# A hybrid token-mixer layer on one core: its opening loads and turns the first token tile earlier, and starts two gates together

## The chip, the core and the metric

The kernel runs on one core of a Trainium2 chip. The metric is the device time of one execution in microseconds (us), the median of the runs shown; lower is better. The core has a matrix engine (TensorE, PE in the profile; its weight loads are the row PEld), a vector engine (VectorE, DVE), an engine for activation functions (ScalarE, ACT), a general engine (GpSimd, POOL) and an engine that only issues transfers (SyncE, SP). Each works through its own instructions in order. Transfers between the chip's main memory and SBUF are issued by an engine's queue and carried out by 16 DMA engines. PE writes to a second on-chip memory, PSUM, in banks of 128 x 512 numbers of 32 bits.

## The reference, cut to what matters

Two groups of tokens, 2048 sample tokens and 128 prompt tokens of width 1024, pass through one layer with shared weights. Around the change the reference computes

```
m = silu(cvec) @ w_ada + b_ada          # one conditioning vector per group, w_ada is 1024 x 3072
shift, scale, gate = split(m, 3)
xn = rmsnorm(h, ln_g) * (1 + scale) + shift
proj = xn @ w_in                        # 7696 columns: qkv, beta, dec, z_a, u_b, v_b, z_b, x_c, z_c, gates
```

and later uses silu(z_a), 512 columns of the projection, as the gate of the first mixer branch. Behind it stand that branch (a gated DeltaNet in both directions in chunks), a spatial gating branch, a Fourier branch, the projections that merge them, the output projection, a gated residual and a last norm.

## The kernel before, in words

All large products are made of three products of 16-bit numbers: each operand is held as a high and a low half (`w.hi`, `w.lo`; `xh`, `xl`), and hi x hi, hi x lo and lo x hi are summed in PSUM. The scaled and shifted tokens are kept on chip, transposed (channels on the partitions), as `xh` and `xl`. Tokens are worked in five tiles (`TBS`): four of 512 sample tokens, numbered 0 to 3, and one of 128 prompt tokens; the contraction over 1024 channels runs in 8 steps of 128 (`KT`).

**The modulation** (L398 to L411). `w_ada`'s columns for shift and scale come in 8 blocks of 256 columns, each as two loads of 512 KB (tile `ast`, 8 buffers). PE multiplies them by the two conditioning vectors (`mm` at L161); in the blocks 0, 2, 4 and 6 (`AD`) the second half is summed by VectorE instead (`ada_sum`, L380 and L382) and then added over partitions by PE with the selector `sel`. The result, 2 x 256, is copied out (L409) and turned to columns by PE (L411) in the PSUM tile `pa`. Behind block 3 (`XB = 4`) the load of the first token tile (`load_x`, L389, 2 MB) and the small parameters (`columns`, L355 to L363) are issued. With all eight blocks there, L415 to L426 add the bias, form `ms` (scale) and `sh` (shift), derive from bounds on both a power-of-two factor `sx` and its inverse `isx` (`scales`, L178 to L188, whose PE matmul at L181 adds over the partitions), and multiply by it.

**A weight block** of 128 columns (512 KB, tile `wst`, two buffers) is loaded by `read_w` (L195) and converted by `converting` (L198 to L219): ScalarE squares it with a sum (L209), VectorE casts the sum (L175), PE adds it over partitions (L181), VectorE forms the factor (L183 to L187) and `w.inv`, the product of the inverse factor and `isx` (L216), ScalarE writes `w.hi` (L218) and VectorE `w.lo` (L219). `wlist` holds the order of the blocks, the four of z_a first; `weight_step` takes one step of the conversion in hand, `fetch` raises the count that may be begun, `getw` steps until blocks are done and `read_next` issues a load ahead.

**A token tile** (L438 to L466). ScalarE squares its rows with sums (L447), VectorE and GpSimd form the reciprocal root (L170, L171), VectorE scales the rows (L451). For each k PE transposes four 128 x 128 blocks (L455) into a bank, VectorE scales and shifts them to the 32-bit tile `xm` (L457), ScalarE casts that to `xh` (L458), GpSimd subtracts to `xl` (L459). Then for each of the four z_a blocks `gemm_T` (L230) runs the 8 steps of three matmuls, ScalarE takes a sigmoid (L464), VectorE the product (L465), and the result goes to main memory one group late (L467). The next stage is the q, k and v projection with its convolution.

**What sets the order.** A scheduler orders every engine's instructions ahead of the run by simulating their time, with the program's order as priority. `tc.high_priority()` raises it; `tc.issue_after(i)` keeps instructions behind the instruction i in that order. On the chip each engine then follows its fixed order and waits on semaphores. SP's queue holds nearly all loads of the opening. A tile taken from a pool waits until the last use of the buffer that it takes over.

## Time and profile before

| what | value |
|---|---|
| median of 3 runs | 2199.03 us (2198.21 to 2199.14) |
| span of the profiled execution, first to last instruction | 2198.9 us |
| the same execution's time around the span | not shown apart from the runs' times; the median is 0.1 us above the span |
| PE busy in the span | 2133.4 us, 97% |
| DVE, ACT, POOL busy | 1297.7, 1007.5 and 713.8 us |
| mean granted PE clock | 0.994 |
| read from main memory, written | 234.67 MB, 127.62 MB |

Views used below: the page; a table by stretch (its length, then busy time of each engine with the count of instructions, the granted PE clock as a share of full speed, the mean busy share of the DMA engines and GB/s); instructions in order of time (start, length, engine, line, operation, output <- inputs, and in brackets the idle time before it and what ended it); groups of instructions by line and form (count, busy us, mean ns of one, idle time before and its cause); DMA issues (count, KB each, median us from issue to landing). PE's matmuls are pipelined, so the distance of two starts says more than the length of one.

### The profile page before, as it was taken

To read this page: it belongs to the slowest core of one execution; us is meant where nothing else is said; L and a number is where in the kernel's file an instruction comes from. 1 tells how busy PE (TensorE), PEld (TensorE's weight loads), DVE (VectorE), ACT (ScalarE), POOL (GpSimd) and SP (SyncE) were. 2 spreads that over 40 slices of the span, in tenths; PEclk is the share of its full clock that TensorE was granted. 3 is DMA by queue.
4 is the path that set the end of the run, shared out by engine and by line. 5 is a ranking of instruction groups with operands and counts; after the bars stand their busy time and mean duration, and the time that the engine had idled before them with its cause. 6 is when DMAs were issued, how large, how long until landed. Compare 5 with 4: busy or idle time off the path is not lost.

```text
span 2198.9 us, 41979 instructions
## 1 busy us (share of the span) xinstructions
PE 2133.4 (97%) x15990; PEld 1231.3 (56%) x15990; DVE 1297.7 (59%) x3085; ACT 1007.5 (46%) x2325; POOL 713.8 (32%) x861
## 2 busy tenths in 40 slices
...
GB/s 279 142 99 156 252 117 111 60 206 220 238 224 237 205 166 110 123 115 115 219 171 165 161 168 187 235 186 212 213 207 147 172 125 123 124 101 110 180 153 105
DMA packets 304275, 365.04 MB, mean 166 GB/s; under 512 B 39393, under 2 KB 215754, under 8 KB 302026
## 3 DMA queue, kind: packets, MB, share of 16 engines
...
q14 instruction: 76, 0.62, 0.1%
HBM read 234.67 MB, written 127.62 MB: 165 GB/s over the span
## 4 chain that ended last, share of the span: by engine, by line
PE 47%; DMA 6%; DVE 5%; ACT 3%; issue 1%; POOL 1%; SPq 0%; ACTq 0%; POOLq 0%; DVEq 0%
PE b L161 47%; DMA st<-br 2%; DMA wst<-in_w_branch_dram 1%; DMA wst<-in_w_in_dram 1%; DMA mt<-mrg 1%; DVE E L788 1%; DVE XB L787 1%; DMA ei<-XB 0%; DMA skn<-kv 0%; DMA br<-o 0%; ACT big L1336 0%; DMA XB<-nd 0%; ACT XB L793 0%; DVE big L1337 0%; DVE u L904 0%
## 5 line engine op out<-in xcount | busy, mean ns | idle before, releaser
L161 PE MATMUL b<-xh,whi 128*128 128x512 f16 (+1 forms) x1920 | 650.5, 347 | 7.7 <-DVE sg L1125 5.0
L161 PE MATMUL b<-xl,whi 128*128 128x512 f16 (+1 forms) x1920 | 650.8, 347 | 0.0
L161 PE MATMUL b<-xh,wlo 128*128 128x512 f16 (+1 forms) x1920 | 650.2, 347 | 0.4 <-DVE wlo L219 0.4
L161 PEld LDWEIGHTS <-whi 128*128 128x128 f16 x3904 | 356.4, 98 | 335.2 <-issue 13.7
L161 PEld LDWEIGHTS <-wlo 128*128 128x128 f16 x1952 | 191.1, 98 | 178.8 <-issue 1.3
L161 PE MATMUL b<-big,bhi 128*128 128x512 f16 (+1 forms) x960 | 250.5, 347 | 1.5 <-DVE big L1337 1.1
L1376 POOL TENSOR_TENSOR mrow<-mrow,sg 128x512 f32<-128x512 f32 (+1 forms) x80 | 95.0, 1187 | 288.4 <-DVE sg L1375 163.6
L161 PE MATMUL b<-big,blo 128*128 128x512 f16 (+1 forms) x480 | 163.3, 347 | 0.0
L1366 ACT ACTIVATE sg<-b,winv 128x512 f32<-128x512 f32 (+1 forms) x120 | 74.2, 619 | 153.9 <-PE b L161 153.4
L628 POOL TENSOR_TENSOR cy<-cy,raw 128x545 f32<-128x545 f32 (+1 forms) x48 | 74.5, 1580 | 184.4 <-ACT raw L627 184.4
L161 PEld LDWEIGHTS <-xh 128*128 128x128 f16 x1496 | 117.1, 98 | 29.9 <-issue 1.5
L161 PEld LDWEIGHTS <-bhi 128*128 128x128 f16 x960 | 87.0, 98 | 76.0 <-ACT big L1336 0.3
L175 DVE CAST wscb<-wss 128x1 bf16<-128x1 f32 x93 | 14.3, 154 | 190.9 <-ACT wlo L209 83.4
L1375 DVE SCALAR_TENSOR_TENSOR sg<-b,binv,sg 128x512 f32<-128x512 f32 (+1 forms) x80 | 53.4, 668 | 102.3 <-PE b L161 90.9
L860 POOL COPY T<-ES 32x256 f16<-32x256 f16 x68 | 28.5, 419 | 208.2 <-DMA ES<-ei 179.3
L161 PE MATMUL b<-whi,xl 128*128 128x128 f16 x544 | 93.0, 219 | 0.0
L161 PE MATMUL b<-whi,xh 128*128 128x128 f16 x544 | 93.0, 219 | 0.0
L161 PE MATMUL b<-wlo,xh 128*128 128x128 f16 x544 | 93.0, 219 | 0.0
L161 PE MATMUL b<-wohi,mh 128*128 128x512 f16 (+2 forms) x248 | 91.9, 372 | 0.6 <-ACT mh L1446 0.6
L161 PE MATMUL b<-wohi,ml 128*128 128x512 f16 (+2 forms) x248 | 91.7, 372 | 0.3 <-DVE ml L1447 0.3
L161 PE MATMUL b<-wolo,mh 128*128 128x512 f16 (+2 forms) x248 | 91.9, 372 | 0.0
L219 DVE SCALAR_TENSOR_TENSOR wlo<-wst,wsc,whi 128x1024 f16<-128x1024 f32 x52 | 72.4, 1396 | 31.6 <-ACT whi L218 31.3
(455 smaller groups left out, 4281.2 us busy)
## 6 DMA issues: line engine op xcount, KB each, us to landing
wst<-in_w_in_dram SPq DMA_DIRECT2D x60, 512.0 KB, 5.5
...
st<-br SPq DMA_DIRECT2D x48, 256.0 KB, 4.6
mrow<-mrg SPq DMA_DIRECT2D x18, 512.0 KB, 4.0
...
dc<-dec SPq DMA_DIRECT2D x17, 512.0 KB
kq<-qkv SPq DMA_DIRECT2D x34, 256.0 KB, 4.8
```

Source lines behind the costliest of these rows:

```text
L161: PE.matmul(out, l, r, start=start, stop=stop)
L175: V.tensor_copy(sb16, ss)
L219: V.scalar_tensor_tensor(w.lo, st, s, w.hi, ALU.mult, ALU.subtract)
L628: G.tensor_tensor(y[:, c0:c1], y[:, c0:c1], raw[:, 1 + c0:1 + c1], ALU.mult)
L787: V.tensor_tensor(t3, X3[:, 0:k, k:k + 1].to_broadcast([P, k, n_]), E3[:, k:k + 1, k:32].to_broadcast([P, k, n_]), ALU.mult)
L788: V.tensor_tensor(E3[:, 0:k, k:32], E3[:, 0:k, k:32], t3, ALU.subtract)
L860: G.tensor_copy(T16[rows(a0, b), :, :, b], ES[0:32, :, 2 * a0 + b, :, wT])
L1366: A.activation(sg, ps, AF.Sigmoid, scale=gw.inv)
L1375: V.scalar_tensor_tensor(sg, ps, binv[:, 1:2], sg, ALU.mult, ALU.mult)
L1376: G.tensor_tensor(mr, mr, sg, ALU.add)
```

## The change

1. The first load of constants is cut to the identity (128 of 778 columns); the rest is loaded later, behind the second token tile. The load of w_spatial is kept behind that too.
2. The order of loads becomes: three modulation blocks, token tile 0 and the small parameters, three modulation blocks, the first two z_a weight blocks, the last two modulation blocks, then z_a blocks 2 and 3, token tile 1, the other constants, the beta and dec columns.
3. Token tile 0 is normalised behind modulation block 5 and transposed (`turn_first`) through the three banks of `ps_mm`; ScalarE copies each bank, still without scale and shift, to `raws`, in four freed `ast` buffers.
4. The z_a blocks 0 and 1 are converted without `isx` (`w.own`); `w.inv` is formed once `isx` is there.
5. `xh` is written by ScalarE from the transposed block itself, with scale and shift, beside VectorE's `xm`; in tile 0 every second `xl` is subtracted by VectorE.
6. In tile 0 the z_a blocks 0 and 1 go together, with the contraction outermost (`silu_za(0, (0, 1), others)`): six matmuls at each k. The conversions of blocks 2 and 3 are kept behind k = 3 of the tile's `xh` and `xm`, and the matmuls of k = 6 and 7 behind the matmul that sums block 3's squares. Blocks 2 and 3 then follow one by one, and tile 1's normalisation behind block 3's `w.hi`.
7. The square of the shift's bound moves ahead of the scale's.

```diff
--- before.py
+++ after.py
@@ -32,7 +32,6 @@
 QUOTA = 1.6
 SCAN = 1.3
 MT = 0.015
-XB = 4
 AD = (0, 2, 4, 6)
 CQ = 545
 FS = 4096.0
@@ -149,7 +148,7 @@
     cs_ = ExitStack()
     csp = pool(cs_, "csp", 1, side="right")
     cst = sb(csp, [P, _CF], "cst")
-    SY.dma_start(cst, consts[:, 0:_CF])
+    SY.dma_start(cst[:, 0:P], consts[:, 0:P])
     K = {n_: cst[:, a:b] for n_, (a, b) in _COFF.items() if b <= _CF}
     ident, ones = K["ident"], K["ones"]
     ones16 = sb(cp, [P, P], "ones16", BF16)
@@ -158,7 +157,7 @@
     G.memset(mhalf, -0.5)
 
     def mm(out, l, r, start=True, stop=True):
-        PE.matmul(out, l, r, start=start, stop=stop)
+        return PE.matmul(out, l, r, start=start, stop=stop)
 
     def mm3(out, l, r):
 
@@ -169,6 +168,8 @@
     def rsqrt(out, ss, mul, w):
         V.tensor_scalar(out, ss, mul, EPS, ALU.mult, ALU.add)
         G.tensor_tensor(out, out, mhalf.to_broadcast([P, w]), ALU.pow)
+
+    last_sum = [None]
 
     def widened(ss, pl, tag):
         sb16 = sb(pl, [P, 1], tag + "b", BF16)
@@ -178,7 +179,7 @@
     def scales(ss, pl, tag, sb16=None):
 
         ps = bank(ps_x, [P, 1])
-        mm(ps, ones16, widened(ss, pl, tag) if sb16 is None else sb16)
+        last_sum[0] = mm(ps, ones16, widened(ss, pl, tag) if sb16 is None else sb16)
         t = sb(pl, [P, 4], tag)
         V.tensor_copy(t[:, 0:1], ps)
         h = t[:, 3:4].bitcast(I32)
@@ -192,8 +193,10 @@
 
     def read_w(src, nkt, cols=P, tag="w"):
         st = sb(wp, [P, nkt, cols], "wst" if cols == P else tag + "st", bufs=2 if cols == P else 1)
-        SY.dma_start(st, src.rearrange("(k p) c -> p k c", p=P))
+        last_read[0] = SY.dma_start(st, src.rearrange("(k p) c -> p k c", p=P))
         return st
+
+    last_read = [None]
 
     def converting(w, st, nkt, cols=P, hi=None, lo=None, tag="w", bufs=5):
 
@@ -213,9 +216,12 @@
             yield
         s, inv = scales(None, wp, "wsc", sb16)
         w.inv = sb(wp, [P, 1], "winv", bufs=10)
-        V.tensor_mul(w.inv, inv, isx)
+        if isx is None:
+            w.own = inv
+        else:
+            V.tensor_mul(w.inv, inv, isx)
         yield
-        A.activation(w.hi, st, AF.Copy, scale=s)
+        w.made = A.activation(w.hi, st, AF.Copy, scale=s)
         V.scalar_tensor_tensor(w.lo, st, s, w.hi, ALU.mult, ALU.subtract)
 
     def convert(st, nkt, *args, **kw):
@@ -382,17 +388,44 @@
                     V.scalar_tensor_tensor(acc[:, g, :], st[:, i, :], scT[:, k, g:g + 1], acc[:, g, :], ALU.mult, ALU.add)
 
     pa = bank(ps_x, [P, 16, 2])
-    xts = {}
+    isx = None
+    xts, xss_, raws = {}, {}, []
 
     def load_x(t0, tn):
         xt = sb(p0p, [P, tn // P, D], "xt")
         SY.dma_start(xt, xrows(t0, tn).rearrange("(j p) d -> p j d", p=P))
         xts[t0] = xt
 
+    def normed(t0, nt):
+
+        xt = xts[t0]
+        jk = sb(p0p, [P, D], "jk", F16, bufs=1)
+        xss = sb(p0p, [P, nt], "xss")
+        for j in range(nt):
+            A.activation(jk, xt[:, j, :], AF.Square, accum_out=xss[:, j:j + 1])
+        rs = sb(p0p, [P, nt], "rs")
+        rsqrt(rs, xss, 1.0 / D, nt)
+        for j in range(nt):
+            V.tensor_scalar(xt[:, j, :], xt[:, j, :], rs[:, j:j + 1], None, ALU.mult)
+
+    def turn_first():
+
+        for k in range(KT):
+            ps = bank(ps_mm, [P, 4 * P])
+            for j in range(4):
+                PE.transpose(ps[:, j * P:(j + 1) * P], xts[0][:, j, k * P:(k + 1) * P], ident)
+            if k % 2 == 0:
+                raws.append(sb(p0p, [P, 4, 256], "ast", bufs=8).rearrange("p a b -> p (a b)"))
+            A.copy(raws[-1][:, k % 2 * 512:k % 2 * 512 + 512], ps)
+
+    early = []
     for blk in range(8):
-        if blk == XB:
+        if blk == 3:
             load_x(*TBS[0])
             columns()
+        if blk == 6:
+            read_next()
+            read_next()
         ps = bank(ps_d, [2, 256])
         for k0 in range(0, KT, 4):
             st = sb(p0p, [P, 4, 256], "ast", bufs=8)
@@ -409,63 +442,107 @@
         V.tensor_copy(adr, ps)
         for k in range(2):
             PE.transpose(pa[:, blk * 2 + k, :], adr[:, k * P:(k + 1) * P], ident[:2, :2])
+        if blk == 5:
+            normed(0, 4)
+    fetch(2)
+    while len(wdone) - len(wsteps) < 2:
+        weight_step()
+    turn_first()
     ms = sb(cp, [P, KT, 2], "ms")
     sh = sb(cp, [P, KT, 2], "sh")
     with tc.high_priority():
         spread = lambda a, b: pc[:, a:b].rearrange("p (k o) -> p k o", o=1).to_broadcast([P, KT, 2])
+        bnd = sb(cp, [P, 2, 2 * KT], "bnd")
+        bss = sb(cp, [P, 3], "bss")
         V.tensor_tensor(sh, pa[:, 0:8, :], spread(49, 57), ALU.add)
+        A.activation(bnd[:, 1, :], sh.rearrange("p k g -> p (k g)"), AF.Square, scale=math.sqrt(2.0), accum_out=bss[:, 1:2])
         V.tensor_tensor(ms, pa[:, 8:16, :], spread(57, 65), ALU.add)
         V.scalar_tensor_tensor(ms, ms, 1.0, spread(0, 8), ALU.add, ALU.mult)
-        bnd = sb(cp, [P, 2, 2 * KT], "bnd")
-        bss = sb(cp, [P, 3], "bss")
         A.activation(bnd[:, 0, :], ms.rearrange("p k g -> p (k g)"), AF.Square, scale=math.sqrt(2.0 * D), accum_out=bss[:, 0:1])
-        A.activation(bnd[:, 1, :], sh.rearrange("p k g -> p (k g)"), AF.Square, scale=math.sqrt(2.0), accum_out=bss[:, 1:2])
         V.tensor_add(bss[:, 2:3], bss[:, 0:1], bss[:, 1:2])
         sx, isx = scales(bss[:, 2:3], cp, "xsc")
         V.tensor_scalar(ms, ms, sx, None, ALU.mult)
         V.tensor_scalar(sh, sh, sx, None, ALU.mult)
+        for w in wdone:
+            V.tensor_mul(w.inv, w.own, isx)
 
 
     szD = dram("sz", [H, P, NTOK])
     with tc.issue_after(last_ada.ins):
         read_next()
         read_next()
+    with tc.issue_after(last_read[0].ins):
         load_x(*TBS[1])
-        zaw = getw(4)
-        bdp = sb(wp, [P, KT, 32], "bdp", F16, bufs=1)
-        bdw = load_w(w_in_[:, C_BD:C_BD + 16], KT, 16, hi=bdp[:, :, 0:16], lo=bdp[:, :, 16:32], tag="d")
+        behind = SY.dma_start(cst[:, P:_CF], consts[:, P:_CF])
     szlate = []
-    for ti, (t0, tn) in enumerate(TBS):
-        if t0 not in xts:
-            load_x(t0, tn)
-        g = 0 if t0 < NS else 1
-        nt = tn // P
-        xt = xts[t0]
-        jk = sb(p0p, [P, D], "jk", F16, bufs=1)
-        xss = sb(p0p, [P, nt], "xss")
-        for j in range(nt):
-            A.activation(jk, xt[:, j, :], AF.Square, accum_out=xss[:, j:j + 1])
-        rs = sb(p0p, [P, nt], "rs")
-        rsqrt(rs, xss, 1.0 / D, nt)
-        for j in range(nt):
-            V.tensor_scalar(xt[:, j, :], xt[:, j, :], rs[:, j:j + 1], None, ALU.mult)
-        for k in range(KT):
-            ps = bank(ps_d, [P, tn])
-            for j in range(nt):
-                PE.transpose(ps[:, j * P:(j + 1) * P], xt[:, j, k * P:(k + 1) * P], ident)
-            t = sb(p0p, [P, tn], "xm", bufs=3)
-            V.tensor_scalar(t, ps, ms[:, k, g:g + 1], sh[:, k, g:g + 1], ALU.mult, ALU.add)
-            A.copy(xh[:, k, t0:t0 + tn], t)
-            G.tensor_tensor(xl[:, k, t0:t0 + tn], t, xh[:, k, t0:t0 + tn], ALU.subtract)
-        for g in range(4):
-            ps = bank(ps_d if tn == P and g % 2 else ps_mm, [P, tn])
-            gemm_T(ps, zaw[g], 0, xh[:, :, t0:t0 + tn], xl[:, :, t0:t0 + tn])
+    zaw = []
+
+    def silu_za(ti, gs, between=None):
+
+        t0, tn = TBS[ti]
+        pss = [bank(ps_d if tn == P and g % 2 else ps_mm, [P, tn]) for g in gs]
+        rh, rl = xh[:, :, t0:t0 + tn], xl[:, :, t0:t0 + tn]
+        if len(gs) == 1:
+            gemm_T(pss[0], zaw[gs[0]], 0, rh, rl)
+        else:
+            for k in range(KT):
+                if k == 6:
+                    between()
+                with tc.issue_after(last_sum[0].ins) if k == 6 else ExitStack():
+                    for g, ps in zip(gs, pss):
+                        mm(ps, zaw[g].hi[:, k, :], rh[:, k, :], k == 0, False)
+                        mm(ps, zaw[g].lo[:, k, :], rh[:, k, :], False, False)
+                        mm(ps, zaw[g].hi[:, k, :], rl[:, k, :], False, k == KT - 1)
+        for g, ps in zip(gs, pss):
             sg = sb(ep, [P, tn], "sg", bufs=4)
             A.activation(sg, ps, AF.Sigmoid, scale=zaw[g].inv)
             V.scalar_tensor_tensor(sg, ps, zaw[g].inv, sg, ALU.mult, ALU.mult)
             if szlate:
                 SY.dma_start(*szlate.pop())
             szlate.append((szD[g, :, t0:t0 + tn], sg))
+
+    for ti, (t0, tn) in enumerate(TBS):
+        if t0 not in xts:
+            load_x(t0, tn)
+        g = 0 if t0 < NS else 1
+        nt = tn // P
+        if ti == 1:
+            with tc.issue_after(zaw[3].made.ins), tc.issue_after(first_t.ins):
+                normed(t0, nt)
+        elif ti:
+            normed(t0, nt)
+        for k in range(KT):
+            if ti:
+                src = bank(ps_d, [P, tn])
+                for j in range(nt):
+                    PE.transpose(src[:, j * P:(j + 1) * P], xts[t0][:, j, k * P:(k + 1) * P], ident)
+            else:
+                src = raws[k // 2][:, k % 2 * 512:k % 2 * 512 + 512]
+            t = sb(p0p, [P, tn], "xm", bufs=3)
+            hi = A.activation(xh[:, k, t0:t0 + tn], src, AF.Identity, scale=ms[:, k, g:g + 1], bias=sh[:, k, g:g + 1])
+            of = V.tensor_scalar(t, src, ms[:, k, g:g + 1], sh[:, k, g:g + 1], ALU.mult, ALU.add)
+            (V if ti == 0 and k % 2 else G).tensor_tensor(xl[:, k, t0:t0 + tn], t, xh[:, k, t0:t0 + tn], ALU.subtract)
+            if k == 3:
+                half_hi, half_t = hi, of
+        if ti == 0:
+            first_t = of
+            zaw.extend(wdone[:2])
+
+            def others():
+                with tc.issue_after(half_hi.ins), tc.issue_after(half_t.ins):
+                    zaw[2:] = getw(4)[2:]
+
+            silu_za(0, (0, 1), others)
+            bdp = sb(wp, [P, KT, 32], "bdp", F16, bufs=1)
+            with tc.issue_after(behind.ins):
+                bdst = read_w(w_in_[:, C_BD:C_BD + 16], KT, 16, "d")
+            with tc.issue_after(zaw[3].made.ins):
+                bdw = convert(bdst, KT, 16, hi=bdp[:, :, 0:16], lo=bdp[:, :, 16:32], tag="d")
+            silu_za(0, (2,))
+            silu_za(0, (3,))
+        else:
+            for g in range(4):
+                silu_za(ti, (g,))
     SY.dma_start(*szlate.pop())
     p0.close()
     ahead(2)
@@ -630,7 +707,8 @@
             if ct < 4 or ct > 7:
                 A.activation(raw[:, 1:LP - 1], y, AF.Square, accum_out=vqs[:, ct:ct + 1])
     wsn = sb(ep, [P, WB], "st", bufs=3).rearrange("p (g q) -> p g q", g=4)
-    SY.dma_start(wsn, w_spatial[0].rearrange("g p q -> p g q"))
+    with tc.issue_after(behind.ins):
+        SY.dma_start(wsn, w_spatial[0].rearrange("g p q -> p g q"))
     pace.drain()
     a1.close()
```

## The prediction

> **What bounds the kernel now.** I read the page first, then a table of engine time by stage, then the opening by two-microsecond slices, then its instructions in order of time. From the page only the span:
>
> ```profile
> span 2198.9 us, 41979 instructions
> ```
>
> The table by stage (stretch, length, busy time of PE, PEld, DVE, ACT and POOL, granted clock, DMA share, GB/s) shows where PE, the matrix engine, is not busy:
>
> ```profile
> 0.00:64.00 64.00, 46.85 (x218) 21.29 (x219) 36.16 (x93) 23.06 (x43) 14.84 (x19) 0.92 0.85 275
> 64.00:160.00 96.00, 96.00 (x580) 52.70 (x579) 54.69 (x105) 48.04 (x86) 35.57 (x41) 1.00 0.35 113
> 160.00:500.00 340.00, 339.02 (x2122) 175.01 (x2119) 203.44 (x338) 173.52 (x311) 101.52 (x115) 1.00 0.46 150
> 500.00:1600.00 1100.00, 1060.99 (x9728) 691.99 (x9727) 733.11 (x1888) 568.23 (x1516) 372.46 (x513) 1.00 0.60 183
> ```
>
> PE is full from 64 to 500 us and idles 39 us of the 1100 that follow. Before 64 us it idles 17 us, and much of what counts as busy there is modulation, not projection. The change touches that stretch and, lightly, the four token tiles behind it. If PE is full from the end of the opening on, a microsecond won there is a microsecond off the end.
>
> What holds the opening is first the DMA queue of SP:
>
> ```profile
> 24.00:26.00 2.00, 1.01 (x3) 0.34 (x4) 0.23 (x1) 1.94 (x5) 0.00 (x0) 0.56 0.83 242
> ...
> 32.00:34.00 2.00, 2.00 (x11) 0.68 (x8) 1.47 (x5) 0.00 (x0) 0.00 (x0) 1.00 1.12 353
> 34.00:36.00 2.00, 0.42 (x3) 0.20 (x2) 2.00 (x6) 0.00 (x0) 0.00 (x0) 1.00 1.10 328
> 36.00:38.00 2.00, 1.93 (x10) 0.71 (x10) 0.57 (x2) 0.00 (x0) 0.00 (x0) 1.00 1.21 292
> 38.00:40.00 2.00, 2.00 (x13) 1.03 (x14) 0.00 (x0) 0.67 (x1) 0.00 (x0) 1.00 1.11 281
> ...
> 46.00:48.00 2.00, 0.67 (x3) 0.67 (x4) 2.00 (x11) 1.87 (x2) 0.00 (x0) 0.50 0.01 1
> 48.00:50.00 2.00, 2.00 (x11) 1.62 (x10) 2.00 (x4) 2.00 (x5) 1.10 (x1) 0.50 0.00 0
> 50.00:52.00 2.00, 1.90 (x8) 0.79 (x6) 2.00 (x3) 2.00 (x5) 2.00 (x2) 0.62 0.32 58
> ```
>
> The DMA share is above 1 and about 350 GB/s flow; where the weight blocks pass (36 to 40 us) it is about 285. By 46 us nothing flows: loading is over, and a chain of dependent steps runs. That chain, in order of time (start, length):
>
> ```profile
> 36.07 1.89 PE L161 MATMUL b<-ast,scT 128*2 128x256 f32 x8 [1.65 <-DMA ast<-in_w_ada_dram]
> ...
> 41.06 1.06 ACT L209 ACTIVATE zlo<-wst 128x1024 f16<-128x1024 f32 x1 [0.59 <-DMA wst<-in_w_in_dram]
> ...
> 42.25 0.16 DVE L175 CAST wscb<-wss 128x1 bf16<-128x1 f32 x1 [1.58 <-ACT zlo L209]
> 42.32 0.73 DVE L409 COPY adr<-b 2x256 f32<-2x256 f32 x2
> ...
> 46.01 0.14 DVE L187 TENSOR_SCALAR wsc<-wsc 128x1 int32<-128x1 int32 x1
> ...
> 46.20 0.23 DVE L426 TENSOR_SCALAR sh<-sh,xsc 128x16 f32<-128x16 f32 x1
> ...
> 49.09 0.63 PE L161 MATMUL b<-xh,zhi 128*128 128x512 f16 x1
> ```
>
> The last modulation copy (L409, 42.32) stands on VectorE behind the cast of the second gate weight's sum (L175), which waits for ScalarE's square, which waits for that weight's DMA (41.06). So the second weight, not the modulation matrix, releases the modulation. Scale and shift are ready at 46.43, and the first projection matmul starts at 49.09. From there PE waits for the tile itself. Grouped by form, 44 to 64 us (count, then busy time and mean ns):
>
> ```profile
> L459 POOL TENSOR_TENSOR xl<-xm,xh 128x512 f16<-128x512 f32 x8 | 12.1, 1526 | 19.5 <-ACT xh L458 19.5
> ...
> L455 PE MATMUL b<-cst,xt 128*128 128x128 f32 x33 | 6.3, 332 | 2.8 <-DVE wsc L186 2.6 <-issue 0.3
> ...
> L161 PE MATMUL b<-xh,zhi 128*128 128x512 f16 x15 | 5.4, 413 | 0.0
> L161 PE MATMUL b<-xl,zhi 128*128 128x512 f16 x14 | 5.3, 394 | 0.5 <-POOL xl L459 0.4
> L161 PE MATMUL b<-xh,zlo 128*128 128x512 f16 x13 | 4.9, 379 | 0.0
> ...
> L458 ACT CAST xh<-xm 128x512 f16<-128x512 f32 x8 | 4.8, 606 | 0.0
> ```
>
> And the end of the thin stretch, with the pace that follows:
>
> ```profile
> 62.93 0.55 PE L455 MATMUL b<-cst,xt 128*128 128x128 f32 x3 [0.94 <-DVE wsc L186]
> ...
> 63.77 0.38 PE L161 MATMUL b<-xh,zhi 128*128 128x512 f16 x1
> 63.98 0.38 PE L161 MATMUL b<-xl,zhi 128*128 128x512 f16 x1
> ```
>
> ```profile
> 77.33 1.25 PE L455 MATMUL b<-cst,xt 128*128 128x128 f32 x10
> ```
>
> 42 projection matmuls start by 64 us; the last four lie behind 63.3 us, so 38 are done there. Dense, one starts every 0.216 us (63.77 to 63.98), and ten transposes take about 1.1. Besides, nine transposes of the second tile are done by 63.3 (33 here and 8 before 44, less the first tile's 32). That is 38 x 0.216 + 9 x 0.11 = 9.2 us of dense PE work, spread over the 14.2 us from 49.09. This point, 63.3 us with 9.2 us of work done, is my yardstick.
>
> **The change, part by part.** *Bytes ahead of the modulation.* Sizes (KB each, median us to landing):
>
> ```profile
> ast<-in_w_ada_dram SPq DMA_DIRECT2D x16, 512.0 KB, 5.1
> xt<-in_x_sample_dram SPq DMA_DIRECT2D x4, 2048.0 KB, 12.8
> wst<-in_w_in_dram SPq DMA_DIRECT2D x10, 512.0 KB, 8.0
> ...
> cst<-in_consts_dram SPq DMA_DIRECT2D x1, 389.0 KB
> st<-in_w_spatial_dram SPq DMA_DIRECT2D x1, 256.0 KB
> ```
>
> Two weight blocks (+1024 KB) now go ahead of the last four modulation loads; 325 KB of constants (128 of 778 columns stay in front) and the 256 KB of w_spatial move behind. Net +443 KB, 1.3 us at 350 GB/s; 1024 KB at 285 instead of 350 costs 0.7 more. The last loads' matmuls waited until 36.07 in before; one more block follows, 1.5 us at 350 GB/s, so the last landed near 37.6. After: 37.6 + 2.0 = 39.6; the slice of 242 GB/s at 24 us, which a gapless queue would not have, may give back 0.6. I take 39.0.
>
> *From there to the first matmul.* The last half block is 8 matmul records, 1.9 us (row at 36.07): 40.9. Its copy finds VectorE free, since the weights' sums are done earlier: no 0.9 us wait. In before the chain from that copy to the end of L426 is 46.43 - 42.32 = 4.1 us with two copies of 0.37; with one it is 3.8: 44.7. The square of the shift moves ahead of the scale's, which is 0.2 us of ScalarE off this chain or nothing. Then ScalarE makes xh directly, 0.6 us (L458's 606 ns; from a source in SBUF with two column operands unknown, between that and 0.7). First projection matmul: 44.7 + 0.6 = 45.3, less 0.4 for the weights' steps that VectorE now does in between (five like that at 46.01, an estimated 0.07 us each): **44.9**, against 49.09.
>
> *Tile 0 turned early.* Its 32 transposes leave the path, and eight ScalarE copies, 0.6 us each, are added; they run near 29 to 37 us, where ScalarE shows no work at all (0.00 in the rows 32 to 36), so they cost nothing; without that cover 4.8 us. The tile lands sooner than now, because six modulation loads stand ahead of it instead of eight.
>
> *Contraction outermost, two gates.* Each slice k feeds six matmuls, 1.30 us of PE, and needs one ScalarE pass (0.6), one VectorE pass and one subtraction, taken in turn by POOL (1.2 to 1.5) and VectorE. Both engines finish a pair of slices in under the 2.6 us that PE needs. So from 44.9 PE goes at its own pace: 9.2 us of work. Two subtractions remain. First, PE idles some 4 us before 44.9, as it does in before, where the rows 46 to 50 show a granted clock of 0.50 and the row 50 to 52 a mean of 0.62, so full speed comes some 2.4 us past 49.09. At half clock for 3.4 us that is 1.7 us lost. (TensorE: Matmul & The Clock Gate in the Trainium skill, section "Part 1: The HAM clock gate", says that after an idle window of about 3.4 us the array runs at half rate until about as long of activity; the rows here agree, and by that rule the loss is an estimated 1.7 us too, against 0 if the clock stayed.) Second, VectorE's pass now reads SBUF. How such a pass fares beside POOL:
>
> ```profile
> 60.72 1.60 POOL L459 TENSOR_TENSOR xl<-xm,xh 128x512 f16<-128x512 f32 x1
> 61.23 1.64 DVE L451 TENSOR_SCALAR xt<-xt,rs 128x1024 f32<-128x1024 f32 x1
> ...
> 62.98 0.74 DVE L451 TENSOR_SCALAR xt<-xt,rs 128x1024 f32<-128x1024 f32 x1
> ```
>
> The same instruction takes 0.74 us alone and 1.64 beside POOL. Half that size is 0.4 alone, so if the two exclude each other a pair of slices takes 2 x 0.4 + 0.7 + 1.2 = 2.7 us instead of 1.5, just over PE's 2.6. I charge 0.5 us in all (bounds 0 and 4 x 1.2 = 4.8, each POOL pass fully in the way). (SBUF — State Buffer in the Trainium skill, "Who interferes with whom", calls it an exclusive lock held for the whole instruction; it speaks against this change, which moves a PSUM reader to SBUF. By it the sum loses an estimated 0.5 to 1 us, without it nothing.)
>
> *Weights 2 and 3* wait for the two staging buffers, which come free when weights 0 and 1 are converted, now possible before the modulation. I put that at 40 to 41 us (ScalarE: copies to 37, then 4 passes of about 1.1); landing 8 us later at 49, sums at 51. PE reaches k = 6, where it is made to stand behind them, at 44.9 + 1.7 + 7.8 = 54.4. Cover 3 us; past it each microsecond costs one. The second token tile is queued on SP behind these two: it lands near 50 instead of 46, needs an estimated 12 us (four squares like that at 41.06, four scalings, the first turns), and is wanted near 71 (46.6 + 96 x 0.216 + 32 x 0.11). The rest of the constants and w_spatial are queued behind that and read well past 100 us: nothing. Tiles 1 to 4 give ScalarE a PSUM source, VectorE the same; PE has 20 us of work per tile: nothing, bounds -1 and +2.
>
> *Sum.* 44.9 + 9.2 + 1.7 + 0.5 = 56.3 us for the work that stood done at 63.3: **7.0 us** gained. Span 2198.9 - 7.0 = 2191.9; the median of the runs shown is 2199.03, 0.1 above the span. I predict **2192.0 us**.
>
> **The rivals.** *Weights late.* If VectorE's last conversion slips behind the modulation chain (to 46 us), the two weights land at 54 to 55, the sums come at 57, PE stands 2.6 us at k = 6 and the second tile comes at about 73, in time. 2194.6 to 2196. For: VectorE and ScalarE are in-order, and in before a cast did just this to L409. Against: the conversions need only DMA. *The change does not do what it says*: the early turn ends after the modulation, for its eight copies share ScalarE with squares and conversions, and PE again waits for them; gain 0 to 3 us, 2196 to 2199. *Slower: the middle is ordered anew.* The program's order on every engine is fixed by a planner that simulates time, and the opening shifts its engines unequally. The dear place is 500 to 1600 us, for example this stretch of PE, and the wait in it on the chain of waits:
>
> ```profile
> 800.00:900.00 100.00, 92.31 (x887) 0.99 0.33 88
> ```
>
> ```profile
> 842.83 10.02 DMA ei<-XB
> ```
>
> PE loses 7.7 us of those 100, with a 10 us transfer in the chain. One more such stretch eats the gain (2199.6); from two on the kernel is slower: 2192 + 15.4 = 2207. For: 39 us of stalls lie there. Against: the filling work in between is unchanged and the shift is 0.3% of the span. It may equally lose a stall.
>
> **How the numbers follow.** Forecast 0.60, weights late 0.14, no early turn 0.09, one new stall 0.09 (2197 to 2202), two or more 0.08. What a measurement of this kernel can tell from no change is about 0.2%, 4.4 us. Below 2194.6: most of the forecast and a third of the late weights, 0.66; within 4.4 us: 0.26; slower by more: 0.08. The range: the low end takes no clock loss, no port loss, the first matmul at 43.9 and one or two microseconds of stalls gone (7 + 1.7 + 0.5 + 1 + 2 = 12): 2186.5. The high end takes in late weights and no early turn, and most of one new stall: 2199.5.
>
> **What would show it.** Right: first projection matmul at 44 to 46 us, no wait of L409's successor for a weight's square, 32 transposes before 38 us, PE without gaps above 0.5 us behind 47 us, slow clock for the first 2 to 4 us of it, and each later landmark (first matmul of tile 1, end of the gate stage, the stage table's rows) about 7 us sooner. Wrong: a wait of PE on a weight's sum at k = 6 or on the second tile; the modulation ready later than 45 us; or an unchanged gain at 160 us that is gone by 1600, which would be the planner.

## The result, and the profile after

| kernel | median of its runs (range) | before, beside it | ratio, 95% interval |
|---|---|---|---|
| after, first set | 2209.87 us of 4 (2206.88 to 2213.85) | 2199.09 of 4 | 1.0043 [1.0025, 1.0062] |
| after, second set | 2209.22 us of 11 (2205.55 to 2216.5) | 2202.16 of 28 | 1.0032 [1.0020, 1.0044] |

The change makes the kernel slower, by 7 to 11 us. The forecast was 2192.0, faster by 7. In the sets of ten runs and more one kernel spreads over 8 to 14 us (the kernel before: 2194.86 to 2208.59 in a set of 29), and the profiles' time behind the opening differs by as much; totals alone tell little here, so I looked for a landmark.

**The landmark.** It is the start of the fourth eviction (ScalarE's copy of a finished product out of PSUM) of the convolution stage, called L4. Before, then after (first profiled execution), from the timeline:

```profile
183.04 0.69 ACT L619 ACTIVATE raw<-b,winv 128x512 f32<-128x512 f32 x1 [2.91 <-PE b L161]
```

```profile
194.88 0.69 ACT L696 ACTIVATE raw<-b,winv 128x512 f32<-128x512 f32 x1 [2.91 <-PE b L160]
```

Ahead of it PE has done the same work in every kernel of this study: 160 gate matmuls of each of the three forms, 136 turns (transposes) of tokens, 136 pairs of the beta and dec columns, 33, 32 and 32 of the next weights. Only e10, f3 and g1 below add 32, 32 and 16 turns. One group of that count, before and after:

```profile
L161 PE MATMUL b<-xh,zhi 128*128 128x512 f16 (+1 forms) x160 | 51.5, 350 | 0.0
```

```profile
L160 PE MATMUL b<-xh,zhi 128*128 128x512 f16 (+1 forms) x160 | 54.6, 361 | 5.8 <-ACT xh L522 3.7 <-DVE sg L499 2.1
```

So L4 can be split into four terms: the start of the first projection matmul, the time behind it in which PE idles, the time lost to a slow clock, and work, which is what is left. Idle and clock are summed over two-microsecond slices (2 less PE's busy time; busy time by one less the granted clock).

| us | first matmul | idle | clock | work | L4 |
|---|---|---|---|---|---|
| before | 49.1 | 1.7 | 1.2 | 131.1 | 183.0 |
| after, first profile | 52.2 | 6.7 | 5.8 | 130.2 | 194.9 |
| after, second profile | 48.3 | 7.1 | 3.0 | 130.7 | 189.1 |

The spans less L4 are 2015.9 us before, 2017.2 and 2018.3 after: most of the loss is ahead of L4. The table by stage of the first profile says the same, in the columns of the one shown for before:

```profile
0.00:64.00 64.00, 49.74 (x216) 20.14 (x217) 34.61 (x97) 25.04 (x42) 7.22 (x14) 0.95 0.84 275
64.00:160.00 96.00, 89.47 (x443) 45.61 (x441) 51.60 (x94) 50.80 (x84) 33.61 (x28) 0.95 0.31 102
160.00:500.00 340.00, 339.26 (x2197) 177.73 (x2196) 199.81 (x316) 168.98 (x294) 93.15 (x124) 1.00 0.45 147
500.00:1600.00 1100.00, 1063.57 (x9648) 691.31 (x9647) 734.28 (x1895) 570.54 (x1528) 368.62 (x507) 0.99 0.60 183
```

PE, which was full from 64 us on, now idles 6.5 us in the 96 that follow, and the middle is as it was (36 us idle of 1100; 39 before).

**Where it idles.** PE's waits, second profile (start, length, what, and in brackets the wait before it and who ended it):

```profile
46.17 0.16 PE L160 MATMUL b<-xscb,ones 128*128 128x1 bf16 x1 [1.28 <-DVE xscb L176]
48.27 0.59 PE L160 MATMUL b<-xh,zhi 128*128 128x512 f16 x1 [1.94 <-ACT xh L522]
72.32 2.54 PE L518 MATMUL b<-cst,xt 128*128 128x128 f32 x12 [1.34 <-DVE xt L409]
76.20 0.81 PE L160 MATMUL b<-xh,zhi 128*128 128x512 f16 x3 [1.35 <-ACT xh L522]
78.72 0.59 PE L160 MATMUL b<-xl,zhi 128*128 128x512 f16 x1 [1.01 <-POOL xl L524]
100.94 0.38 PE L160 MATMUL b<-xh,zhi 128*128 128x512 f16 x1 [2.00 <-DVE sg L499]
```

Two holes: tile 1 is not there at 72 us, and at 101 a gate waits for the bank that an older product still holds. Behind the first the clock is 0.64 and 0.51 (rows 78 to 82). ScalarE's queue shows why (second profile):

```profile
58.30 2.19 ACT L224 ACTIVATE zhi<-wst,wsc 128x1024 f16<-128x1024 f32 x2 [3.06 <-DVE wsc L187]
...
60.68 1.04 ACT L405 ACTIVATE jk<-xt 128x1024 f16<-128x1024 f32 x1
...
67.42 1.06 ACT L212 ACTIVATE wlo<-wst 128x1024 f16<-128x1024 f32 x1 [0.66 <-DMA wst<-in_w_in_dram]
68.47 0.67 ACT L498 ACTIVATE sg<-b,winv 128x512 f32<-128x512 f32 x1
69.04 1.04 ACT L405 ACTIVATE jk<-xt 128x1024 f16<-128x1024 f32 x1
...
97.19 1.06 ACT L405 ACTIVATE jk<-xt 128x1024 f16<-128x1024 f32 x1 [2.08 <-DMA xt<-in_x_sample_dram]
98.38 1.06 ACT L405 ACTIVATE jk<-xt 128x1024 f16<-128x1024 f32 x1
99.43 1.25 ACT L498 ACTIVATE sg<-b,winv 128x512 f32<-128x512 f32 x2
```

The first of tile 1's four squares (L405) starts at 60.68, behind the conversions of weights 2 and 3 (L224), and the fourth at 69.04, behind squares of the next weights (L212) that wait for their loads. The change itself holds them there (`tc.issue_after(zaw[3].made.ins)`). And at 97.19 a square of tile 3, which waits for a load, stands ahead of the sigmoids that free the banks.

**The modulation.** PE ahead of the first projection matmul, second profile:

```profile
33.97 0.66 PE L416 MATMUL b<-cst,xt 128*128 128x128 f32 x4
34.46 0.17 PE L160 MATMUL b<-wscb,ones 128*128 128x1 bf16 x1
34.55 1.89 PE L160 MATMUL b<-ast,scT 128*2 128x256 f32 x8
36.37 1.53 PE L416 MATMUL b<-cst,xt 128*128 128x128 f32 x12
38.21 0.28 PE L444 MATMUL b<-cst,adr 2*128 2x2 f32 x2 [0.30 <-DVE adr L442]
38.42 2.32 PE L160 MATMUL b<-ast,scT 128*2 128x256 f32 x10
...
43.70 0.33 PE L416 MATMUL b<-cst,xt 128*128 128x128 f32 x1
44.27 0.61 PE L444 MATMUL b<-cst,adr 2*128 2x2 f32 x4 [0.24 <-DVE adr L442]
```

PE has no wait above 0.3 us from 29 to 44 us. Loading pauses at 37 with all of the modulation there, and PE still has 7 us of work, some 2 of them turns of tile 0 (the rows of 1.53, 0.55 and 0.33). It is no longer a last load that sets the modulation, as the second weight's did in before, but PE's own queue. In the first profile a gap in the loads comes on top (162 GB/s from 20 to 22 us, where the second has 339):

```profile
34.34 3.54 PE L160 MATMUL b<-ast,scT 128*2 128x256 f32 x8 [1.80 <-DMA ast<-in_w_ada_dram]
...
52.18 0.58 PE L160 MATMUL b<-xh,zhi 128*128 128x512 f16 x1 [1.94 <-ACT xh L522]
```

Behind the wait that follows from it the granted clock is 0.58 and 0.57 (rows 34 to 38), eight matmuls take 3.54 us instead of 1.89, and everything behind is 4 us later; that belongs to the execution, as the second profile shows.

### The profile page after: what moved, and what is told of

It is laid out like the page before. It is cut to its first block, busy times and chain, and to the rows that moved or that the text cites. A ratio compares the mean times of both kernels' runs of the same rounds, so it can differ in the third digit from the quotient of the medians.

```text
span 2212.1 us, 41999 instructions
## 1 busy us (share of the span) xinstructions
PE 2145.3 (97%) x15990; PEld 1234.0 (56%) x15990; DVE 1300.3 (59%) x3089; ACT 1016.7 (46%) x2333; POOL 699.7 (32%) x857
## 4 chain that ended last, share of the span: by engine, by line
PE 45%; DMA 6%; DVE 6%; ACT 3%; issue 1%; POOL 1%; SPq 0%; ACTq 0%; POOLq 0%; DVEq 0%
PE b L160 44%; DMA wst<-in_w_in_dram 2%; DMA wst<-in_w_branch_dram 1%; DMA st<-br 1%; DVE E L866 1%; DVE XB L865 1%; DMA ei<-XB 0%; DVE wlo L225 0%; DMA br<-o 0%; DVE big L1415 0%; DMA skn<-kv 0%; DMA of<-sz 0%; DMA mrg<-mrow 0%; DMA wst<-mrg 0%; ACT big L1414 0%
## 5 line engine op out<-in xcount | busy, mean ns | idle before, releaser
L705 POOL TENSOR_TENSOR cy<-cy,raw 128x545 f32<-128x545 f32 (+1 forms) x48 | 65.2, 1385 | 185.5 <-ACT raw L704 185.5
L212 ACT ACTIVATE wlo<-wst 128x1024 f16<-128x1024 f32 x52 | 54.9, 1056 | 78.1 <-DMA wst<-in_w_in_dram 67.7
```

The lines of the kernel that those rows point to most:

```text
L212: A.activation(w.lo, st, AF.Square, accum_out=ss)
L705: G.tensor_tensor(y[:, c0:c1], y[:, c0:c1], raw[:, 1 + c0:1 + c1], ALU.mult)
```

## The experiments

The theories. **A**: the loss is waits in the fixed order of in-order engines (late modulation, tile 1's hold, tile 3's square). **B**: tile 1's load comes too late. **C**: the pile on PE (modulation matmuls and turns still to be done when the loads are there) is the same whatever the order of loads. **D**: the new tile path itself loses (ScalarE making xh from PSUM at 0.78 us, against a cast of 0.61). **P**: PE bounds the opening, so early turns delay the modulation. **H**: the early turns are hidden beside the loads, as predicted. **W**: a busy wait keeps PE's clock.

| run | first matmul | idle | clock | work | L4 | ratio to before, 95% |
|---|---|---|---|---|---|---|
| e1_free | 49.6 | 5.1 | 1.5 | 130.2 | 186.4 | 1.0028 [1.0009, 1.0046] |
| e2_x1early | 48.6 | 8.0 | 4.2 | 130.7 | 191.5 | 1.0029 [1.0014, 1.0043] |
| e4_wlate | 49.1 | 4.7 | 4.3 | 130.1 | 188.2 | 1.0025 [1.0009, 1.0040] |
| e5_turnlate | 46.9 | 11.8 | 2.4 | 130.9 | 192.0 | 1.0056 [1.0034, 1.0078] |
| e7_free_sq | 48.9 | 6.3 | 4.6 | 131.2 | 191.0 | 1.0034 [1.0022, 1.0046] |
| e8_wlate_sq | 50.9 | 7.9 | 2.9 | 130.9 | 192.6 | 1.0045 [1.0032, 1.0058] |
| e9_wearly_sq | 51.2 | 7.1 | 1.4 | 130.9 | 190.6 | 1.0032 [1.0020, 1.0044] |
| b3_tilepath | 47.7 | 4.7 | 1.7 | 132.8 | 187.0 | 1.0023 [1.0011, 1.0034] |
| e10_turn2 | 51.4 | 4.0 | 1.7 | 130.4 | 187.5 | 0.9999 [0.9987, 1.0011] |
| e11_sq3 | 48.6 | 3.3 | 1.7 | 129.7 | 183.3 | 1.0010 [0.9997, 1.0024] |
| e13_turnlate_sq3 | 47.6 | 8.2 | 4.5 | 130.2 | 190.5 | 1.0025 [1.0011, 1.0040] |
| e15_half_sq3 | 48.7 | 2.3 | 1.7 | 129.8 | 182.5 | 1.0003 [0.9992, 1.0014] |
| f1_after | 48.3 | 7.1 | 3.0 | 130.7 | 189.1 | 1.0032 [1.0020, 1.0044] |
| f2_sq3 | 49.7 | 4.9 | 3.2 | 130.4 | 188.3 | 1.0011 [1.0000, 1.0022] |
| f3_sq3_turn2 | 50.0 | 3.0 | 0.0 | 129.8 | 182.7 | 0.9994 [0.9982, 1.0005] |
| g1_half_warm | 50.1 | 5.7 | 2.3 | 129.6 | 187.6 | 1.0013 [0.9999, 1.0026] |

The terms are of one profile each, the ratios of all runs. The two profiles of the changed kernel differ by 3.9 us in the first matmul and by 5.8 in L4, so a difference of a microsecond or two between two rows shows nothing by itself. The profiled execution was the fastest of all for e9, e11 and b3, the slowest for e7 and e10. All are edits of the changed kernel but b3, which is one of the kernel before.

**e1_free**: tile 1's hold off.

```diff
-        if ti == 1:
-            with tc.issue_after(zaw[3].made.ins), tc.issue_after(first_t.ins):
-                normed(t0, nt)
-        elif ti:
+        if ti:
             normed(t0, nt)
```

> The changed kernel, but token tile 1 is normalised as soon as it is there, not behind the conversion of z_a block 3. Theory A (orders): the opening's loss has three parts, the modulation 6.5 us later than forecast, a hole of PE of 7.3 us in front of tile 1 because ScalarE's squares are held behind block 3, and a wait of 2.1 us with a slow clock behind it at 105 us. Without the hold the hole goes: 2199 to 2204 us, and the fourth eviction of the convolution stage (183.0 us in before, 194.9 in the changed kernel) comes at 184 to 189. Theory B (load): tile 1 is late because its load stands behind z_a blocks 2 and 3 on SP; then nothing moves: 2208 to 2212, and 194 to 196.

The hole before tile 1 is nearly gone (1.65 us at 63 in place of some 4 at 70 to 80), with the load of tile 1 where it was. Against the second profile of after L4 is 2.7 us earlier, at 186.4, where A had it. The total does not show it: the median is 2209.74, against A's 2199 to 2204, and within B's range.

**e2_x1early**: the hold kept, tile 1 loaded ahead of weights 2 and 3.

```diff
-    with tc.issue_after(last_read[0].ins):
+    with tc.issue_after(last_ada.ins):
         load_x(*TBS[1])
+    with tc.issue_after(last_read[0].ins):
         behind = SY.dma_start(cst[:, P:_CF], consts[:, P:_CF])
```

> The changed kernel, but tile 1 is loaded right behind the modulation, ahead of z_a blocks 2 and 3; the hold on its normalisation stays. Theory A: the load was there at about 54 us and the squares began at 64.4, so an earlier load gives nothing, and later blocks 2 and 3 cost up to 2 us: 2208 to 2213, fourth eviction 194 to 197. Theory B: tile 1 turns 6 us sooner: 2201 to 2205.

Tile 1's load is issued at 30.1 us instead of 43.2 (second profile of after), and the hole stays (waits of 2.24, 1.35 and 1.01 us from 74.7 on). B falls: it is the hold, not the load.

**e4_wlate**: weights 0 and 1 loaded behind all modulation loads.

```diff
-        if blk == 6:
-            read_next()
-            read_next()
...
+    with tc.issue_after(last_ada.ins):
+        read_next()
+        read_next()
     fetch(2)
```

> The changed kernel, but z_a blocks 0 and 1 are loaded behind all the modulation loads. Theory A: the last modulation matmuls wait for a load that stands behind those two blocks, and PE then works off what piled up; without that scale and shift are ready at 45 to 47 us instead of 51.2, the first projection matmul comes at 47 to 49 instead of 52.2, and the total is 3 to 5 us lower, 2205 to 2207. Rival C: the pile of PE work (modulation, early transposes) is the same whatever the load order; scale and shift come at 50 to 51 and the total stays.

PE's wait for loads between 28 and 44 us is gone, but the conversions of the weights now stand in the scale's chain on ScalarE and VectorE, and the first projection matmul comes at 49.1 all the same (scale and shift at 48.1, between A and C). The order of loads moves the pile from one queue to another and shortens nothing, which speaks for C and against that part of A.

**e5_turnlate**: tile 0 turned behind the modulation.

```diff
-            PE.transpose(pa[:, blk * 2 + k, :], adr[:, k * P:(k + 1) * P], ident[:2, :2])
+            last_turn = PE.transpose(pa[:, blk * 2 + k, :], adr[:, k * P:(k + 1) * P], ident[:2, :2])
...
-    turn_first()
+    with tc.issue_after(last_turn.ins):
+        turn_first()
```

> The changed kernel, but tile 0 is transposed behind the last modulation matmuls. Theory A: 14 of the 32 early transposes and their copies stand in front of the modulation's last matmuls on PE; with them behind, scale and shift come at 48 to 49.5 us instead of 51.2. The copies then lie on the path of the tile, so the first projection matmul gains less, 50 to 53, and the total is within 2 us of the changed kernel, 2208 to 2212. Rival: the early turn itself is worth its forecast 4 us; then putting it back costs that: 2212 to 2215.

Scale and shift are ready at 45.3, the first projection matmul starts at 46.9, the earliest of all: without the turns in PE's queue scale and shift come 2.0 us sooner than in f1, the changed kernel's second profile (47.3). That contradicted what I had put down for A. The total, 2214.25, is where the rival had it, but not for its reason: the gain is lost behind the first matmul, in waits for products of 2.34 us at 68.8 and 2.96 at 80.4. Tile 1's hold is not their cause, for e13 has them without it.

**e7, e8, e9**: tile 1's hold replaced by one behind tile 0's last ScalarE pass, and the squares of tiles 2 to 4 held too; e8 with e4's order of loads, e9 with weights 0 and 1 right behind tile 0.

```diff
+            sigm.setdefault(ti, []).append(A.activation(sg, ps, AF.Sigmoid, scale=zaw[g].inv))
...
+        if ti > 1:
+            with tc.issue_after(sigm[0][1].ins if ti == 2 else sigm[ti - 1][0].ins):
+                normed(t0, nt)
+        elif ti:
+            with tc.issue_after(first_h.ins), tc.issue_after(first_t.ins):
+                normed(t0, nt)
...
+            first_h, first_t = hi, of
```

> Edit to the changed kernel: tile 1's squares stand behind tile 0's last ScalarE pass and no longer behind the conversion of gate weight 3; tile 2's squares stand behind tile 0's second sigmoid, those of tiles 3 and 4 behind the first sigmoid of the tile before. Landmark L4 is the start of the fourth eviction of the convolution stage (183.0 before, 194.9 after, 186.4 with tile 1's hold off alone). Theory A (the loss is waits that stand in the fixed order of in-order engines): with no square waiting for a token load in front of a sigmoid, the waits of TensorE on sigmoid products (1.0 at 98 us) and the idle 3.4 us of 64 to 160 us go to under 1.5; L4 183 to 185, ratio 0.999 to 1.002. Theory D (rival: the loss sits in the new tile path itself, ScalarE making xh from PSUM at 0.77 us beside VectorE, in every tile): no change against the kernel with the hold off alone, L4 186 to 188, ratio about 1.003.

> As the run with all squares placed, and besides gate weights 0 and 1 are loaded behind all sixteen modulation loads. Theory A: modulation matmuls end near 41 us, scale and shift ready at 47 to 48.5 (the weights' conversions now fall into that chain), first projection matmul 48 to 49.5, no tile-1 hole; L4 182 to 185, ratio 0.998 to 1.001. Theory D: L4 186 to 188, ratio about 1.003.

> As the run with all squares placed, but gate weights 0 and 1 are loaded right behind tile 0, ahead of all ten remaining modulation loads, and block 2 is not asked for before the last modulation load. Theory A (TensorE's pile of work came from its wait for the one modulation load that stood behind the weights): the ten loads arrive in a row, no pile; scale and shift ready at 45 to 47, first projection matmul 46 to 48, no tile-1 hole; L4 180 to 183, ratio 0.996 to 1.000. Theory C (the pile of matmuls and turns is the same whatever the order of loads): scale and shift at 48 to 51, L4 184 to 187, ratio 1.001 to 1.004.

All three missed what A had. Their ratios are about those of D and C, their L4 (191.0, 192.6, 190.6) is later than either had it, and D's reason is not what the traces show: the wait for a product at 97 us stays in e7 (1.0), and a new hole of 3 us stands at 123 to 130 (in e9 at 125 to 131, with the clock at 0.5 behind it). My own hold, behind the first sigmoid of the tile before, is too late for tile 3. In e9 the first projection matmul comes at 51.2, so the loads in a row did not end the pile: for C.

**b3_tilepath**: on the kernel before, xh from PSUM by ScalarE, gates 0 and 1 of tile 0 contraction outermost, every second subtraction on VectorE.

```diff
+            A.activation(xh[:, k, t0:t0 + tn], ps, AF.Identity, scale=ms[:, k, g:g + 1], bias=sh[:, k, g:g + 1])
             V.tensor_scalar(t, ps, ms[:, k, g:g + 1], sh[:, k, g:g + 1], ALU.mult, ALU.add)
-            A.copy(xh[:, k, t0:t0 + tn], t)
-            G.tensor_tensor(xl[:, k, t0:t0 + tn], t, xh[:, k, t0:t0 + tn], ALU.subtract)
+            (V if ti == 0 and k % 2 else G).tensor_tensor(xl[:, k, t0:t0 + tn], t, xh[:, k, t0:t0 + tn], ALU.subtract)
+        pair = [bank(ps_mm, [P, tn]) for _ in range(2)] if ti == 0 else []
+        for k in range(KT if pair else 0):
+            for ps, w in zip(pair, zaw):
...
```

> One part of the change alone, on the kernel before: xh made by ScalarE from PSUM in all tiles, every other subtraction of tile 0 on VectorE, gates 0 and 1 of tile 0 with the contraction outermost; loads, modulation and turns as before. Theory A (the tile path costs nothing or gains a little, the orders of the opening lose): L4 180 to 183.5, ratio 0.998 to 1.000. Theory D (the tile path loses): L4 187 or later, ratio 1.002 to 1.005.

D's numbers came (187.0, 1.0023), though the first matmul is 1.4 us earlier. PE's waits:

```profile
65.94 0.39 PE L161 MATMUL b<-xh,zlo 128*128 128x512 f16 x1 [0.76 <-DVE zlo L219]
73.77 0.63 PE L455 MATMUL b<-cst,xt 128*128 128x128 f32 x4 [1.16 <-DVE wsc L185]
98.26 0.38 PE L161 MATMUL b<-xh,zhi 128*128 128x512 f16 x1 [0.80 <-DVE sg L474]
```

They are waits on steps of weights and on a product, in a newly made order. e11 has the same tile path and an L4 of 183.3: D as a law of this path falls there. For b3 itself D is not excluded by another run.

**e10_turn2**: e1, and each early turn of tile 0 made twice.

```diff
-                PE.transpose(ps[:, j * P:(j + 1) * P], xts[0][:, j, k * P:(k + 1) * P], ident)
+                for again in range(2):
+                    PE.transpose(ps[:, j * P:(j + 1) * P], xts[0][:, j, k * P:(k + 1) * P], ident)
```

> The changed kernel with tile 1's hold off (first projection matmul 49.6, L4 186.4 there), and each of the 32 early transposes of tile 0 made twice. Theory P (the opening is bound by TensorE from about 33 us on, so the early turns stand on the path to the modulation): some 20 to 24 of the 32 stand behind 33 us, and two thirds or more of their 0.14 us each come on top: first projection matmul 52 to 54, L4 189 to 191, ratio 1.004 to 1.006. Theory H (the prediction's: the turns lie hidden beside the loads): first projection matmul 49 to 50, L4 186 to 187, ratio about 1.003.

First projection matmul 51.4, 1.8 us later than e1: between the two. 16 of the 64 turns fell into PE's wait behind the modulation, where they cost nothing; of the 32 added, 16 stood ahead of it, at 0.12 us about 2. L4 is 187.5, near H's. The ratio of 0.9999, better than e1's, neither theory has, and it stays unexplained.

**e11_sq3**: tile 1's squares behind tile 0's last ScalarE pass, tile 3's behind tile 1's third sigmoid (tiles 2 and 4 get tile 1's bound; `sigm` and `first_h` as in e7).

```diff
+        if ti == 3:
+            with tc.issue_after(sigm[1][2].ins):
+                normed(t0, nt)
+        elif ti:
+            with tc.issue_after(first_h.ins), tc.issue_after(first_t.ins):
+                normed(t0, nt)
```

> The changed kernel with tile 1's squares behind tile 0's last ScalarE pass instead of behind weight 3's conversion, tile 2's likewise, and tile 3's squares behind the third sigmoid of tile 1 (no longer behind the first sigmoid of tile 2, which came too late at 123 to 130 us). Theory A (waits in the fixed order): no wait of TensorE on a sigmoid product at 97 to 105 us and none on tile 3's turn near 125; idle behind the first projection matmul under 4 us (5.1 with the hold alone off), L4 184 to 186, ratio 0.999 to 1.002. Theory D (the tile path itself loses): L4 186 to 188, ratio 1.003.

L4 is 183.3, as in before, and the ratio of 1.0010 can no longer be told from 1. Only squares were placed anew, and at the landmark the loss is gone. A wait of 1.0 us for a product at 96 stays, which A did not have.

**e13_turnlate_sq3**: e11 with e5's late turn.

> The kernel with the squares placed, and tile 0 turned behind the last modulation transpose instead of ahead of it. Theory P: the turns then lie in the time in which TensorE waits for the scale's chain, which is free; scale and shift ready at 44.5 to 46, first projection matmul 46 to 47.5 with TensorE kept warm (no half clock, 1.5 us saved), idle 3 to 5 us, L4 181 to 184, ratio 0.996 to 1.000. Theory H (the early turn saves its time): the turns and their copies come on top, first projection matmul 48 to 50, L4 186 to 189, ratio 1.002 to 1.005.

The first matmul comes at 47.6 with PE at full clock, close to what P has; L4 (190.5) and the idle time do not, and the ratio, 1.0025, is in H's range: the new order has waits of 2.04 us at 69 and 2.39 at 81, for products.

**e15_half_sq3**: e11, with half of the turn (16) late.

```diff
-    turn_first()
+    turn_first(range(4))
+    with tc.issue_after(last_turn.ins):
+        turn_first(range(4, KT))
```

> The kernel with the squares placed behind tile 1's third sigmoid (first projection matmul 48.6, L4 183.3, ratio 1.001), and of tile 0's turn only the first half (16 transposes) early; the second half stands on TensorE behind the last modulation transpose, in the time in which TensorE waits for the scale's chain. Theory P (the opening is bound by TensorE behind 33 us, each early transpose there delays the modulation): 16 transposes fewer there, 2 to 2.5 us; scale and shift ready at 45 to 46, first projection matmul 46 to 47.5, TensorE warm when it starts; L4 179.5 to 182, ratio 0.997 to 0.9995. Theory H (the early turn is hidden wherever it stands): first projection matmul 48 to 49.5, L4 183 to 185, ratio 1.000 to 1.002.

It has the least idle time (2.3) and L4 0.8 us ahead of e11, with the ratio at 1. The first projection matmul is not earlier (48.7): PE's queue is 1.3 us shorter between its first turn and the last of the modulation, but in this execution it began 0.9 later, and PE waits 0.8 and 0.5 us for two copies of the modulation on VectorE, the first of them behind a weight's conversion. P in this form is not shown.

**f1_after, f2_sq3, f3_sq3_turn2**: the changed kernel again; the same with tile 3's placement of e11 alone; e11 with doubled turns.

> The changed kernel itself, a second execution under the profile. If the late modulation is the change's: first projection matmul 51.5 to 52.5, L4 194 to 196. If it is one execution's (a gap in the loads at 28 us and half clock at 34 us there): first projection matmul 48.6 to 49.6, and with the waits of 5 to 7 us and the slow clock behind them L4 190 to 192. Ratio 1.003 to 1.005 either way.

> The changed kernel with one edit: tile 3's squares behind the third sigmoid of tile 1; tile 1's squares stay behind weight 3's conversion. Theory A: the wait of 2.1 us on a sigmoid product near 105 us and the half clock behind it go, the hole before tile 1 near 75 us stays; against the changed kernel in the same set L4 is 2 to 4 us earlier, ratio 1.001 to 1.004. Theory D (the tile path itself loses): L4 as in the changed kernel.

> The kernel with the squares of tiles 1, 2 and 3 placed (first projection matmul 48.6, L4 183.3, ratio 1.001), with each of the 32 early transposes made twice. Theory P (TensorE bounds the opening): first projection matmul 50 to 52, L4 184.5 to 187, ratio 1.001 to 1.003. Theory H (the turns are hidden beside the loads): first projection matmul 48.3 to 49.5, L4 183 to 184, ratio 1.000 to 1.0015.

f1 settles the late modulation: of the 7.3 us by which the first profile's first projection matmul missed 44.9, 3.9 were that execution's and 3.4 stay. f2 beside f1: the hole at 101 is gone, the one at 72 to 79 stays, ratio 1.0011 against 1.0032; in L4 it is 0.8 us, less than A had, and 2.2 in L4 less the first matmul. The totals and L4 do not split the loss alike: tile 1's hold off (e1) has the better L4, tile 3's placement (f2) the better ratio. That both placements count is shown by the holes; how much each is worth is open.

f3: the first matmul is at 50.0, 1.4 later than e11, as P has it, but L4 is 0.5 earlier and the ratio 0.9994, where neither theory has them. What pays for it in the profile is the clock: f3 loses nothing to it, e11 1.7 us. The doubled turns are not the reason. f3's rows come first here, then those of e10, which has the same 64 turns and the same wait of 1.97 us ahead of its first projection matmul (columns as in the table by stage):

```profile
46.00:48.00 2.00, 1.99 (x19) 1.89 (x18) 0.75 (x5) 1.52 (x6) 0.00 (x0) 1.00 1.12 311
48.00:50.00 2.00, 0.04 (x1) 0.04 (x1) 1.88 (x11) 1.49 (x3) 0.02 (x1) 1.00 0.98 354
50.00:52.00 2.00, 1.79 (x8) 0.72 (x8) 2.00 (x4) 2.00 (x4) 1.58 (x2) 1.00 1.00 408
```

```profile
46.00:48.00 2.00, 2.00 (x20) 1.82 (x19) 0.41 (x3) 1.43 (x5) 0.00 (x0) 1.00 1.16 302
48.00:50.00 2.00, 1.42 (x14) 1.34 (x13) 0.79 (x7) 1.50 (x5) 0.00 (x0) 1.00 0.95 326
50.00:52.00 2.00, 0.60 (x3) 0.29 (x3) 2.00 (x9) 1.51 (x4) 0.58 (x1) 1.00 1.00 408
52.00:54.00 2.00, 1.79 (x6) 0.62 (x5) 2.00 (x3) 2.00 (x4) 1.57 (x2) 0.71 1.01 398
54.00:56.00 2.00, 2.00 (x6) 0.76 (x5) 2.00 (x4) 2.00 (x4) 1.12 (x2) 0.50 1.24 265
```

Both are busy up to the wait; f3 then runs at full clock, and e10 at half until 56 us. What differs is where the wait falls. In every trace here the clock changes only at points that lie whole multiples of 3.41 us apart within one execution; e10's, found by narrowing the rows, go down at 22.13 and 52.85 and up at 25.54 and 56.26. Counted by these steps, e10's wait lies whole in the one from 49.44 to 52.85, in which PE idles 2.2 us, and f3's is cut at 49.27 into two steps with 1.3 and 0.9 us. Where the steps lie differs between executions, so f3's full clock, and the L4 that goes with it, was luck.

**g1_half_warm**: e15, and 16 turns into a bank that nobody reads, behind the matmul of the scale's sum.

```diff
+        warm = bank(ps_mm, [P, 4 * P])
+        with tc.issue_after(last_sum[0].ins):
+            for i in range(16):
+                j = i % 4
+                PE.transpose(warm[:, j * P:(j + 1) * P], xts[0][:, j, 0:P], ident)
```

> The kernel with half of tile 0's turn behind the modulation (first projection matmul 48.7, clock 0.5 to 0.8 for some 5 us behind it with 1.7 us lost, L4 182.5, ratio 1.0003), with 16 extra transposes, whose result nobody reads, in TensorE's wait behind the matmul of the scale's sum. Theory W (a busy wait keeps the clock): first projection matmul 48.3 to 49.0, granted clock 0.95 or more behind it, lost clock under 0.3 us, L4 180.5 to 181.5, ratio 0.9985 to 1.000. Rival (the clock in that place goes by the load of the whole opening and not by the last 3 us): clock as without them, L4 182 to 183.5, ratio 1.000 to 1.001.

W holds for the clock: 1.00 in every row from 44 to 56 us, although it had been 0.5 at 40. With the wait filled, PE idles 0.3 us at most in a step of 3.41 us from 46 to 56, and e5 and e13, whose turns fill the wait, have 1.00 there too. L4 (187.6) and the ratio (1.0013) are not as W had them: the start came late in this execution (50.1), and the new order has two holes of its own.

```profile
75.44 0.81 PE L160 MATMUL b<-xh,zhi 128*128 128x512 f16 x3 [1.55 <-ACT xh L531]
79.15 1.94 PE L527 MATMUL b<-cst,xt 128*128 128x128 f32 x8 [2.91 <-DVE wsc L186]
```

No version is shown to beat the kernel before; e10, e11, e15, f3 and g1 cannot be told from it.

**Left open.** The part behind L4 took 2010.9 to 2020.5 us in these profiles, with no trend that I can name; so a ratio can stray from its L4, as e10's does. e11's L4 is that of the fastest of its 12 executions. How much of b3's loss is its order and how much chance was not tried further.

## Why the prediction was wrong, point by point

The predicted first projection matmul was 44.9, and from there dense work.

- **The last modulation load at 39.0**: earlier, 37 us (second profile). Right, or better.
- **"From there to the first matmul", the last half block 1.9 us behind the load: this step failed.** It took the modulation as bound by DMA in after because it is in before. PE has 7 us of queued work behind the last load, and the modulation's matmuls end at 43.8, not 40.9. I had counted PE only for the last half block and counted the early turns' cost on ScalarE ("they cost nothing"); that PE issues 32 turns, 4.5 us from start to start, in a queue without a wait above 0.3 us from 29 us on was missing. First matmul 48.3, against 49.1 before: 0.8 us gained, not 4.2. Two pairs that differ in the turn alone bear it out: the modulation's last matmul ends at 43.8 and 41.2 (f1, e5) and at 44.1 and 41.8 (e11, e13). f3 (first matmul 50.0 with the turns doubled) fits; e15 does not decide.
- **Contraction outermost, PE at its own pace**: right. In the second profile 62 projection matmuls have started by 63.3 us (38 and nine turns before); 24 x 0.216 less 9 x 0.11 is 4.2 us ahead. PE does not wait at k = 6, but the cover of 3 us was gone: the sums came at 57.5, when PE was there.
- **Cold clock, 1.7 us**: 1.5 in the second profile, 1.7 in e11. The size is right; whether it is paid is chance, for f3 and e9 had a wait of 1.9 us and more there and lost none behind it. TensorE: Matmul & The Clock Gate in the Trainium skill, section "Part 1: The HAM clock gate", gives an idle window of about 3.4 us. The traces agree with the length of the step, 3.41 us, but a step need not be idle throughout: 2.2 us of idling in one were enough in e10.
- **VectorE beside GpSimd, 0.5 us**: The two do exclude each other: a pass of `xm` took 0.54 us alone and 1.37 to 1.46 beside a subtraction on GpSimd, and each of the latter ended about 0.28 us behind it (second profile). But a pair of slices took 2.35 us, less than PE's 2.6, so PE lost nothing there. The price fell elsewhere: the twelve passes of tile 0 fill VectorE for 9.8 us, and the sums of weights 2 and 3 wait behind them.
- **"The sums at 51", "needs an estimated 12 us and is wanted near 71 (in time)": failed.** The load was in time (e2). The sums came at 57.5, and the squares were late: the diff keeps them behind weight 3's conversion, which stands behind tile 0's eight passes on ScalarE and twelve on VectorE (58.30). I counted the time of tile 1's steps and not what is queued ahead of them. Price in the second profile: 4.1 us of idling at 70 to 80 and 1.4 of clock behind it.
- **Tiles 1 to 4, "nothing, bounds -1 and +2": failed.** A square that waits for tile 3's load stands ahead of sigmoids: 2.0 us at 101 (with the slow clock behind it 3.8 in the first profile).
- **The rivals**: the slower one, the middle ordered anew, named the right mechanism, an order fixed ahead of the run, and the wrong place: the middle is unchanged, the stalls stand at 70 to 101 us. Weights late and no early turn did not come.

The sum, second profile: 4.2 us ahead at 63.3, then 6.1 us of two holes, 1.0 at 152, 1.4 of clock, and 1.3 us at the eight waits in them, where the record of the last matmul or turn overlaps no next one (a turn lasts 0.27 us, from start to start 0.11): 9.8 against, 5.6 net. L4 has 6.1 (189.1 against 183.0); some 0.4 us are not accounted for.

There was also less to win than I thought. Behind its first projection matmul the kernel before loses 1.7 us idle and 1.2 of clock up to L4, that is all. My 9.2 us of work in 14.2 read as 5 us of air; 1.3 of it were 12 turns of tile 0 that start behind 49.09 and that I had left out. They do not vanish when they are moved to a stretch where PE is the bound.
